# Branch A as seven block products, with its weights' forms and the output product's right operands made behind the first FFN, in a hybrid encoder layer

## The chip, the cores and the metric

The kernel runs on one core of one Trainium2 chip. The metric is device time in microseconds (us) for one execution of the whole layer; a run's span is the time from its first to its last instruction, and some microseconds lie around it. Engines are named as the profile names them: PE (TensorE, matrix products), DVE (VectorE), ACT (ScalarE), POOL (GpSimd) and SP (SyncE, which only issues transfers here).

## What is computed

One bidirectional encoder layer on 1024 tokens of width 1024, all in FP32:

```python
h = h + 0.5 * swiglu(rms_norm(h, ffn1_norm), w_gate1, w_up1, w_down1)
u = rms_norm(h, mix_norm)
qa, ka, va, qb, kb, vb, ga, gb = split(u @ w_in)
ya = neighbourhood_attention_2d(qa, ka, va, rpb)     # 8 heads of 64
yb = windowed_gqa_sink(qb, kb, vb, sink)             # 8 heads of 64
merged = sigmoid(ga) * (ya @ w_branch_a) + sigmoid(gb) * (yb @ w_branch_b)
h = h + merged @ w_out
h = h + 0.5 * swiglu(rms_norm(h, ffn2_norm), w_gate2, w_up2, w_down2)
return rms_norm(h, final_norm)
```

The change concerns `ya @ w_branch_a` (1024 tokens, 512 in, 1024 out: "branch A") and `merged @ w_out` (1024 x 1024 x 1024: "the output product").

## The kernel before

**Exact products from rounded operands.** PE multiplies FP32R operands. Each FP32 operand is split in two: ACT casts it to FP32R (hi, L95) and DVE subtracts that from the source (lo, L98). One product is then three matmuls (mm3, L146): hi times hi (L149), hi times lo (L151), lo times hi (L153), all accumulating in one PSUM bank. Such a product always needs a hi and a lo of both sides. The long products (the FFNs, the output product) are done as seven block products of halves with sums and differences of the blocks as operands ("forms", named P1 to P7), so that seven products do the work of eight.

**Stages in the order of the trace.** FFN 1 (the macaron half-step) up to about 432 us; its down product (class Down, L532); a transition; the input projection; from 935 us attention in 64 units (scores, turn, values; loop at L1476), and between the units' matmuls a "filler" (L1321) of gate columns, branch B and the first part of branch A; after 1160.5 us the rest of branch A (L1537); at 1195.94 us the output product (Down with n=4, L1525); then FFN 2 from about 1300 us to the end. PE runs without a break through all of them, taking each product's operands as the other engines make them. Every engine takes its own instructions strictly in the order that the program gives.

**Branch A before.** yA, a [512, 1024] matrix of (channel, token), comes in four row chunks. Each unit writes its outputs to a DRAM buffer or to a tile (L1381 copy on ACT, L1382 and L1392 adds on DVE). Three chunks are fetched back and split whole (L1496, 128x1024 each), the last one in halves (L1394). For each of eight output chunks dc (order p, p+4) branch_a takes four channel chunks times mm3 times two banks of 512 tokens: 24 matmuls of 128x512, 192 in all. Then DVE multiplies by the gate (L1557, twice 512) and adds to branch B's part (L1558, 1024 wide) in merged(dc). combine (L1528) makes the output product's left forms by four DVE operations (L1534) per p and stores them.

**The output product before.** Down.prep (L579) makes one of 28 entries: a left form (from merged or from left_d) and a right form (blocks of w_out, loaded whole to SBUF, with differences at L590 to L595), and splits each: two ACT casts and two DVE subtractions of 512 an entry. Six entries (RING) are prepared ahead. multiply (L616) takes four column groups, twelve matmuls an entry.

**Behind FFN 1.** PE's 153 block products of FFN 1 are numbered down to n=0 at the end. After each, behind_ffn1 (L770) does background work: the weights of branch B (8 pieces), of branch A (8) and of six gate columns (12 halves) are fetched (256 KB), split (ACT L760, DVE L761) into buffers of the ring "hs" (6), and put to DRAM by POOL's queue (two of 256 KB, L768), one piece every third n from n=100. The same hook drives FFN 1's own down product (Down.at_end, L607): its blocks are loaded at n=10 and 6, its first entries made at n=4, 2, 0. SP issues all loads in order; a load that waits for its buffer holds up those behind it.

## Time and profile before

| quantity | value |
|---|---|
| median of 3 runs | 1919.72 us (1918.26 to 1920.03) |
| span of the profiled execution | 1915.6 us; the median lies 4.1 us above it |
| mean granted clock of PE | 0.999 |
| busy share of the span | PE 99%, DVE 76%, ACT 49%, POOL 16% |
| chain that ended last | PE 97%, DVE 1%, DMA 1% |
| moved by DMA | 338.57 MB, mean 177 GB/s |

In the views a row of a timeline has its start, the duration, the engine, the line, the operation, output<-inputs and the shape; the idle time of the engine before it and what released it stand in brackets. A duration covers the whole pass through an engine, and the next instruction can start before it ends: the distance from one start to the next is what an instruction costs in a row of them. Of matmuls above all only that distance counts.

### The profile page before, as it was taken

To read this page: it belongs to the slowest core of one execution; us is meant where nothing else is said; L and a number is where in the kernel's file an instruction comes from. 1 tells how busy PE (TensorE), PEld (TensorE's weight loads), DVE (VectorE), ACT (ScalarE), POOL (GpSimd) and SP (SyncE) were. 2 spreads that over 40 slices of the span, in tenths; PEclk is the share of its full clock that TensorE was granted. 3 is DMA by queue.
4 is the path that set the end of the run, shared out by engine and by line. 5 is a ranking of instruction groups with operands and counts; after the bars stand their busy time and mean duration, and the time that the engine had idled before them with its cause. 6 is when DMAs were issued, how large, how long until landed. Compare 5 with 4: busy or idle time off the path is not lost.

```text
span 1915.6 us, 25959 instructions
## 1 busy us (share of the span) xinstructions
PE 1905.7 (99%) x9044; PEld 1597.7 (83%) x9044; DVE 1451.9 (76%) x2545; ACT 947.5 (49%) x1847; POOL 306.5 (16%) x477
## 2 busy tenths in 40 slices
PE   9999999999999999999999999999999999999998
PEld 7888888888888888898898888888888888888886
DVE  8988766668967778755887997999675566569864
ACT  7533444444446543444888983475333333344453
POOL 0012222214400112211112201010110001005111
PEclk9999999999999999999999999999999999999999
DMA  7256656677354277753648978444432323492341
GB/s 269 95 175 217 231 200 219 205 277 284 115 180 141 105 213 236 226 176 127 176 117 228 283 225 309 171 154 133 142 110 97 118 88 110 157 357 86 119 140 61
DMA packets 174211, 338.57 MB, mean 177 GB/s; under 512 B 17280, under 2 KB 79616, under 8 KB 174080
## 3 DMA queue, kind: packets, MB, share of 16 engines
q1 hardware_dynamic: 140752, 235.18, 37.5%
q0 software_dynamic: 32464, 100.69, 15.6%
q8 instruction: 71, 1.16, 0.3%
q10 hardware_dynamic: 864, 1.05, 0.2%
q14 instruction: 60, 0.49, 0.1%
HBM read 230.43 MB, written 108.19 MB: 177 GB/s over the span
## 4 chain that ended last, share of the span: by engine, by line
PE 97%; DVE 1%; DMA 1%; ACT 0%; issue 0%; POOL 0%; SPq 0%; POOLq 0%; DVEq 0%; ACTq 0%
PE g L149 18%; PE g L153 17%; PE g L151 17%; PE d L153 12%; PE d L151 12%; PE d L149 12%; PE d L1438 2%; PE g L1457 1%; PE d L1417 1%; PE g L1452 1%; PE d L1418 1%; PE d L142 1%; DVE ar L98 0%; DMA fx<-in_xt_dram 0%; DMA fx<-v_d 0%
## 5 line engine op out<-in xcount | busy, mean ns | idle before, releaser
L149 PE MATMUL g<-ar,ws 128*128 128x512 f32 x1064 | 404.6, 393 | 0.0
L151 PE MATMUL g<-ar,ws 128*128 128x512 f32 x1064 | 401.8, 390 | 0.0
L153 PE MATMUL g<-ar,ws 128*128 128x512 f32 x1064 | 400.4, 390 | 0.0
L149 PE MATMUL d<-ar,ws 128*128 128x512 f32 x728 | 281.6, 390 | 0.4 <-ACT ar L908 0.4
L151 PE MATMUL d<-ar,ws 128*128 128x512 f32 x728 | 281.1, 389 | 0.6 <-DVE ar L910 0.6
L153 PE MATMUL d<-ar,ws 128*128 128x512 f32 x728 | 281.2, 389 | 0.0
L153 PEld LDWEIGHTS g<-ar,ws 128*128 128x128 f32 x1064 | 199.6, 188 | 41.6
L151 PEld LDWEIGHTS g<-ar,ws 128*128 128x128 f32 x1064 | 199.6, 188 | 41.0
L149 PEld LDWEIGHTS g<-ar,ws 128*128 128x128 f32 x1064 | 196.6, 188 | 35.9 <-DVE fa L1030 0.3
L332 DVE TENSOR_TENSOR ws<-raw,ws 128x512 fp32r<-128x512 f32 x216 | 147.6, 688 | 92.9 <-ACT ws L325 92.0
L325 ACT CAST ws<-raw 128x512 fp32r<-128x512 f32 x216 | 132.6, 620 | 149.6 <-PE g L153 67.0
L151 PEld LDWEIGHTS d<-ar,ws 128*128 128x128 f32 x728 | 136.7, 188 | 29.8 <-DVE ar L910 1.2
L149 PEld LDWEIGHTS d<-ar,ws 128*128 128x128 f32 x728 | 136.5, 188 | 28.9 <-ACT ar L908 0.9
L153 PEld LDWEIGHTS d<-ar,ws 128*128 128x128 f32 x728 | 136.6, 188 | 28.7 <-DVE ws L332 0.5
L95 ACT CAST ws<-raw 128x512 fp32r<-128x512 f32 x98 | 61.0, 623 | 119.2 <-PE d L153 59.9
L98 DVE TENSOR_TENSOR ws<-raw,ws 128x512 fp32r<-128x512 f32 x98 | 73.2, 747 | 44.3 <-ACT ws L95 44.2
L444 POOL DMA_DIRECT2D hid<-fx x91 | 49.2, 540 | 349.6 <-DVE fx L504 221.6
L98 DVE TENSOR_TENSOR ws<-ar,ws 128x512 fp32r<-128x512 f32 x114 | 93.5, 828 | 14.6 <-ACT ws L95 14.6
L95 ACT CAST ar<-raw 128x512 fp32r<-128x512 f32 (+1 forms) x81 | 54.0, 670 | 83.5 <-PE g L151 51.5
L149 PE MATMUL g<-ws,ws 128*128 128x512 f32 x232 | 90.9, 392 | 0.0
L153 PE MATMUL g<-ws,ws 128*128 128x512 f32 x232 | 90.4, 390 | 0.0
L151 PE MATMUL g<-ws,ws 128*128 128x512 f32 x232 | 90.3, 389 | 0.0
(344 smaller groups left out, 3830.9 us busy)
## 6 DMA issues: line engine op xcount, KB each, us to landing
raw<-hid SPq DMA_DIRECT2D x70, 512.0 KB
hid<-fx POOLq DMA_DIRECT2D x91, 256.0 KB, 2.7
ar<-in_ffn_w_down_dram SPq DMA_DIRECT2D x32, 512.0 KB
raw<-in_ffn_w_up_dram SPq DMA_DIRECT2D x31, 512.0 KB
raw<-in_ffn_w_gate_dram SPq DMA_DIRECT2D x27, 512.0 KB
hid<-fa POOLq DMA_DIRECT2D x51, 256.0 KB, 2.7
ar<-zs_d POOLq DMA_DIRECT2D x48, 256.0 KB, 7.5
raw<-in_w_in_dram SPq DMA_DIRECT2D x20, 512.0 KB
```

The lines of the kernel that those rows point to most:

```text
L95: hi = nc.scalar.copy(dst_hi, src)
L98: (eng or nc.vector).tensor_tensor(dst_lo, src, f32v(dst_hi), op=ALU.subtract)
L142: nc.tensor.transpose(pt[:, c * P:(c + 1) * P], xs[:, (half * 4 + c) * P:(half * 4 + c + 1) * P], ident)
L149: nc.tensor.matmul(b, lhs[0], r[0], start=first, stop=False, **kw)
L151: nc.tensor.matmul(b, lhs[0], r[1], start=False, stop=False, **kw)
L153: nc.tensor.matmul(b, lhs[1], r[0], start=False, stop=last, **kw)
L325: nc.scalar.copy(w[0][:, :512], a)
L332: nc.vector.tensor_tensor(w[0][:, 512:], a, f32v(w[0][:, :512]), op=ALU.subtract)
L444: nc.gpsimd.dma_start(hid[PRODUCTS.index(p), i], src)
L1417: nc.tensor.matmul(b[:, :nw], un["q"][s], un["kd"][s][:, k0 * P:k1 * P], start=True, stop=False)
L1418: nc.tensor.matmul(b[:, :nw], un["q"][s], un["kl"][s][:, k0 * P:k1 * P], start=False, stop=True)
L1438: nc.tensor.transpose(pt[:, i * P:(i + 1) * P], un["pr"][s][:, i * P:(i + 1) * P], ident)
```

## The change

**Branch A in seven products.** The output chunks are taken in four pairs p (dc = p and p+4); tokens, channels and output columns are halved, and a pair takes seven block products of two channel chunks each, with one bank of 512: 7 x 2 x 3 = 42 matmuls of 128x512 a pair, 168 in all instead of 192. The first products (P1, P5 and P2 of p=0 and 1) lie in the filler, as the first part of branch A did; PE's sequence is the same as before up to the attention's tail. The right side now needs forms of yA: 14 splits of 128x512 (form) and 8 differences (minus, L1356 of the changed file) where there were three splits of 1024 and two of 512. A product that several outputs share is kept: ACT copies it from PSUM (a_keep, L1406, 12 times), DVE adds it (a_gate, L1414, 12 times), and then the gate is applied (L1416, 16 times as L1557 before) and merged (L1418, 8 times as L1558 before). combine has moved from L1534 to L1691.

**Weights' forms.** Branch A's weight forms (four pieces a pair) and the 28 right operands of the output product are made and split behind FFN 1 and put to DRAM (wa_d, wo_d). The output product's entries fetch their right operand, hi and lo in one transfer of 512 KB, instead of making it. The background is now a table of what follows each n: branch B and gates every second n from n=108; branch A's from n=67; the output product's from n=44, every 1.34 n, the last near n=6. Three buffers, the two "xs" and the one "gain", go round for the pieces.

The core of the diff:

```diff
+            if self.right is not None:
+                i = (e + self.shift) % self.RING
+                s, t = (ws4(), ws4()) if i < 4 else pair_slots(self.ring[i - 4])
+                nc.sync.dma_start(f32v(t), self.right[PRODUCTS.index(k), p])
+                split(s[:, :512], s[:, 512:], left, None, self.late)
+                self.ent[e] = s, t
+                return
...
+    def split_out(key, src):
+        n = src.shape[1]
+        o = cast[key] = halves_out()[:, :2 * n]
+        pin(nc.scalar.copy(o[:, :n], src))
+        pin(nc.vector.tensor_tensor(o[:, n:], src, f32v(o[:, :n]), op=ALU.subtract))
...
+    def wo_fetch(p):
+        for n, (r0, c0) in dict(B21=(4, 0), B11=(0, 0), B22=(4, 512), B12=(0, 512)).items():
+            wo[n, p] = hs(F32)
+            nc.sync.dma_start(wo[n, p], wout[0][(r0 + p) * P:(r0 + p + 1) * P, c0:c0 + 512])
+    def wo_split(k, p):
+        for d, a, b in dict(P5=(("B11", "B12", "B11"),), P7=(("B12", "B22", "B12"),), P6=(("B11", "B22", "B11"),),
+                            P4=(("B21", "B21", "B11"),)).get(k, ()):
+            pin(nc.vector.tensor_tensor(wo[d, p], wo[a, p], wo[b, p], op=ALU.subtract))
+        split_out((k, p), wo[SOURCE[k], p])
...
+    def wa_split(g, p):
+        lo, hi = slice(0, 256), slice(256, 512)
+        r1, r2 = wa_raw[p, 0], wa_raw[p, 1]
+        if g == 1:
+            q = wa_raw[p, 2] = hs(F32)
+            pin(nc.vector.tensor_tensor(q[:, lo], r2[:, lo], r2[:, hi], op=ALU.add))
+            pin(nc.vector.tensor_tensor(q[:, hi], r1[:, lo], r2[:, lo], op=ALU.subtract))
+        if g == 2:
+            q = wa_raw[p, 2]
+            pin(nc.vector.tensor_tensor(r1[:, lo], q[:, lo], r1[:, lo], op=ALU.subtract))
+            pin(nc.vector.tensor_tensor(r1[:, hi], r1[:, hi], r1[:, lo], op=ALU.subtract))
+        split_out((g, p), (r1, wa_raw[p, 2] if g == 1 else None, r1, r2[:, hi])[g])
...
+    for i in range(NC8 + 2 * len(gates)):
+        for e, f in ((3, wab_put), (2, wab_split), (0, wab_fetch)):
+            later(108 - 2 * i - e, f, i)
+    for p in range(4):
+        later(67 - 5 * p, wa_fetch, p)
+        for g in range(4):
+            later(64 - 5 * p - 5 * g // 4, wa_split, g, p)
+            later(63 - 5 * p - 5 * g // 4, wa_put, g, p)
+    step = [44 - 1.34 * k for k in range(29)]
+    for p in range(4):
+        later(step[7 * p] + 2, wo_fetch, p)
+        for j, k in enumerate(("P2", "P1", "P3", "P5", "P7", "P6", "P4")):
+            later(step[7 * p + j], wo_split, k, p)
+            later(step[7 * p + j] - 1, wo_put, k, p)
...
-        for e, f in ((3, wab_put), (2, wab_split), (0, wab_fetch)):
-            i, k = divmod(100 - e - n, 3)
-            if k == 0 and 0 <= i < 2 * (NC8 + len(gates)):
-                f(i)
+        for f, *a in background.get(n, ()):
+            f(*a)
...
+    def form(k, c, src):
+        h, l = [slot(i)[:, c * 512:c * 512 + 512] for i in FORMS[k]]
+        split(h, l, src, None, True)
+    def forms_first(c):
+        r = mix["ya", c]
+        form("P1", c, r[:, L])
+        minus(r[:, L], r[:, R], r[:, L])
+        form("P5", c, r[:, L])
+    def forms_last(c, k):
+        r, y = mix["ya", c], mix["ya", c + 2]
+        d, a, b, f = dict(P6=(r[:, L], y[:, R], r[:, L], r[:, L]), P7=(r[:, R], y[:, R], r[:, R], r[:, R]),
+                          P4=(y[:, L], y[:, L], r[:, L], y[:, L]), P3=(None, None, None, y[:, R]))[k]
+        if d is not None:
+            minus(d, a, b)
+        form(k, c, f)
...
+    def a_product(p, k):
+        g, f = GROUP[k]
+        w = mix["wa", p, g]
+        n = 256 if g == 3 else 512
+        key = "X" if k == "P2" else "Y" if k in ("P5", "P3") else "W"
+        first = k in ("P1", "P2", "P5")
+        if first:
+            bk[key, p] = bank("d" if key == "Y" else "g")
+        for c in range(2):
+            o = f * 256 + c * P
+            mm3([bk[key, p]], first and c == 0, c == 1, (w[:, o:o + P], w[:, n + o:n + o + P]),
+                [[slot(i)[:, c * 512:c * 512 + 512] for i in FORMS[k]]], skip_group_check=True)
+    def a_keep(p, k):
+        if k == "P1":
+            both = xs4()
+            kept_a[p, "P1"], kept_a[p, "P5"] = both[:, L], both[:, R]
+        elif k == "P6":
+            kept_a[p, "P6"] = hs(F32)
+        nc.scalar.copy(kept_a[p, k], bk["Y" if k == "P5" else "W", p])
+    def a_gate(p, k):
+        key, add, dc, n = dict(P2=("X", "P1", p, L), P7=("W", "P5", p + 4, R), P4=("W", None, p + 4, L), P3=("Y", "P6", p, R))[k]
+        src, r = bk[key, p], mix["ra", dc]
+        if add is not None:
+            t = kept_a[p, add]
+            nc.vector.tensor_tensor(t, src, t, op=ALU.add)
+            src = t
+        nc.vector.scalar_tensor_tensor(out=r[:, n], in0=r[:, n], scalar=1.0, in1=src, op0=ALU.add, op1=ALU.mult)
+        if k in ("P4", "P3"):
+            nc.vector.tensor_tensor(merged(dc), merged(dc), r, op=ALU.add)
...
+        for k, p, g, f in (("P1", 0, 0, "P6"), ("P5", 0, 1, "P7"), ("P1", 1, None, "P3"), ("P5", 1, None, "P4")):
+            a_product(p, k)
+            yield
+            a_keep(p, k)
+            if g is not None:
+                fetch_wa(1, g)
+            forms_last(0, f)
+            if p == 0 and k == "P5":
+                a_fetch(0)
+        a_open(0)
+        for p in range(2):
+            a_product(p, "P2")
+            yield
+            fetch_wa(p, 2)
...
-            fetch_y(512 + min(n - 57, 2) * P)
-        if n in (60, 61, 63):
-            split_y(Y_A[min(n - 60, 2)], 512 + min(n - 60, 2) * P, nc.vector)
+            fetch_ya(min(n - 57, 2))
+        if n in (60, 61):
+            forms_first(n - 60)
+        if n == 63:
+            form("P2", 0, mix["ya", 2][:, L])
...
+    for k in ("P6", "P3", "P7", "P4"):
+        forms_last(1, k)
...
-    down = Down(4, wo[0], 0.5, place, quarter, {k: left_d[i] for i, k in enumerate(("P5", "P6", "P3", "P7"))},
-                loads, (8, 10), late=True)
+    down = Down(4, None, 0.5, {}, quarter, {k: left_d[i] for i, k in enumerate(("P5", "P6", "P3", "P7"))},
+                loads, (8, 10), late=True, right=wo_d)
...
-    for i, dc in enumerate(a_order):
...
+    def both(p, *ks):
+        for k in ks:
+            for q in (p, p + 1):
+                a_product(q, k)
+                if k in ("P1", "P5", "P6"):
+                    a_keep(q, k)
+    def weights(p, g):
+        for q in (p, p + 1):
+            fetch_wa(q, g)
+    weights(0, 3)
+    a_fetch(1)
+    for p in (0, 2):
+        if p:
+            both(p, "P1", "P5")
+            a_open(3)
+            combine(0)
+            both(p, "P2")
+            combine(1)
+        both(p, "P6")
+        if p == 0:
+            a_open(1)
+            weights(2, 0)
+        for q in (p, p + 1):
+            a_gate(q, "P2")
+        both(p, "P3")
+        if p == 0:
+            weights(2, 1)
+        both(p, "P7")
+        if p == 0:
+            weights(2, 2)
+        for q in (p, p + 1):
+            a_gate(q, "P3")
+            a_gate(q, "P7")
+        both(p, "P4")
+        if p == 0:
+            weights(2, 3)
+        for q in (p, p + 1):
+            a_gate(q, "P4")
+            if p == 0:
+                a_fetch(q + 2)
+        if p == 0:
+            a_open(2)
+            for t in range(4):
+                new_fx(t)
             new_ar(2)
-        if i + 1 == NC8:
-            down.prep_until(2)
...
+    down.prep_until(2)
+    for p in (2, 3):
+        combine(p)
```

Three places of the new order, as the engines' queues hold it. A row names the line, operation, output<-inputs and shape, and what it waits for; numbers behind names tell tiles apart. DVE at the end of attention, before. The rows L1382 and L1392 write the last two units' outputs; ar_564 is the lo of the last part of yA (from fx_10503), on which PE's next lo product waits:

```order
L1382 TENSOR_TENSOR s_839_7519<-g_10804,s_839_7519 64x256 [waits Activation_49]
L1392 TENSOR_TENSOR fx_10503<-g_10804,s_839_7519 64x128 [waits DVE_49]
L1392 TENSOR_TENSOR fx_10503<-g_10804,s_839_7519 64x128
L1382 TENSOR_TENSOR s_839_7519<-g_10831,s_839_7519 64x256 [waits Activation_49]
L1392 TENSOR_TENSOR fx_10503<-g_10831,s_839_7519 64x128 [waits DVE_49]
L1392 TENSOR_TENSOR fx_10503<-g_10831,s_839_7519 64x128
L98 TENSOR_TENSOR ar_564<-fx_10503,ar_564 128x512 [waits Activation_49]
L1557 SCALAR_TENSOR_TENSOR raw_10759<-raw_10759,d_10735 128x512 [waits PE_49,Activation_49]
```

The same place in the changed program. ar_4921 and ar_5300 (higher up) hold forms of yA, xs_10960 and xs_11014 are kept products, raw_10991 a gate, and the last row makes P6's form of the second channel chunk from fx_10701:

```order
L98 TENSOR_TENSOR ar_5300<-fx_10744,ar_5300 128x512 [waits Activation_49]
L1540 TENSOR_TENSOR s_887_7717<-g_11025,s_887_7717 64x256 [waits Activation_49]
L1356 TENSOR_TENSOR fx_10744<-fx_10744,raw_10592 128x512
L1550 TENSOR_TENSOR fx_10701<-g_11025,s_887_7717 64x128 [waits DVE_49]
L1550 TENSOR_TENSOR fx_10701<-g_11025,s_887_7717 64x128
L1414 TENSOR_TENSOR xs_10960<-g_11042,xs_10960 128x512 [waits DMASW2_49,PE_49]
L98 TENSOR_TENSOR ar_5300<-fx_10744,ar_5300 128x512 [waits Activation_49]
L1416 SCALAR_TENSOR_TENSOR raw_10991<-raw_10991,xs_10960 128x512 [waits DVE_49,Activation_49]
L1414 TENSOR_TENSOR xs_11014<-g_11051,xs_11014 128x512 [waits PE_49]
L1540 TENSOR_TENSOR s_887_7717<-g_11058,s_887_7717 64x256 [waits Activation_49]
L1550 TENSOR_TENSOR fx_10701<-g_11058,s_887_7717 64x128 [waits DVE_49]
L1550 TENSOR_TENSOR fx_10701<-g_11058,s_887_7717 64x128
L1356 TENSOR_TENSOR raw_10638<-fx_10701,raw_10638 128x512 [waits DVE_49]
```

Between the last units' adds there now stand L1356, a form's lo (L98), two adds of kept products (L1414) and a gate (L1416), ahead of the last unit's add and of the first difference that needs it (raw_10638). On PE its cast is awaited by the first L149 of P6's second chunk (the third L149 row here), twelve rows behind the last unit's values:

```order
L149 MATMUL d_10967<-ar_5300,ws_11049 128x512
L151 MATMUL d_10967<-ar_5300,ws_11049 128x512
L153 MATMUL d_10967<-ar_5300,ws_11049 128x512
L149 MATMUL d_11018<-ar_5300,ws_11067 128x512
L151 MATMUL d_11018<-ar_5300,ws_11067 128x512
L153 MATMUL d_11018<-ar_5300,ws_11067 128x512
L149 MATMUL g_10939<-ar_4921,ws_11049 128x512 [waits Activation_49]
L149 MATMUL g_10995<-ar_4921,ws_11067 128x512
```

DVE where branch A ends and the output product begins, before. ws_11075 and ws_11081 are the lo's of the left forms of the first two entries, ws_11076 and ws_11082 of the right ones; raw_10926 is a gate:

```order
L1558 TENSOR_TENSOR ar_9540<-ar_9540,raw_10892 128x1024 [waits DVE_49]
L1534 TENSOR_TENSOR fa<-ar_9540 128x512 [waits DMASW0_49,DVE_49]
L98 TENSOR_TENSOR ws_11075<-ar_9541,ws_11075 128x512 [waits DMAHW0_49,Activation_49]
L98 TENSOR_TENSOR ws_11076<-ar_10855,ws_11076 128x512 [waits DMAHW6_49,DMAHW1_49,Activation_49]
L98 TENSOR_TENSOR ws_11081<-ar_9541,ws_11081 128x512 [waits DMAHW3_49,Activation_49]
L98 TENSOR_TENSOR ws_11082<-ar_10855,ws_11082 128x512 [waits DMAHW6_49,Activation_49]
L1557 SCALAR_TENSOR_TENSOR raw_10926<-raw_10926,g_11003 128x512 [waits PE_49]
L1557 SCALAR_TENSOR_TENSOR raw_10926<-raw_10926,g_11004 128x512 [waits PE_49]
L1558 TENSOR_TENSOR ar_9541<-ar_9541,raw_10926 128x1024 [waits DVE_49]
```

The same place in the changed program, with the left forms' lo's ws_11328 and ws_11333:

```order
L1418 TENSOR_TENSOR ar_9738<-ar_9738,raw_11181 128x1024 [waits DVE_49]
L1416 SCALAR_TENSOR_TENSOR raw_11183<-raw_11183,xs_11208 128x512 [waits DVE_49,Activation_49]
L1416 SCALAR_TENSOR_TENSOR raw_11177<-raw_11177,g_11192 128x512 [waits PE_49]
L1416 SCALAR_TENSOR_TENSOR raw_11183<-raw_11183,g_11201 128x512 [waits PE_49]
L1418 TENSOR_TENSOR ar_9739<-ar_9739,raw_11177 128x1024 [waits DVE_49]
L1418 TENSOR_TENSOR ar_9739<-ar_9739,raw_11183 128x1024 [waits DVE_49]
L98 TENSOR_TENSOR ws_11328<-ar_9739,ws_11328 128x512 [waits DMAHW0_49]
L98 TENSOR_TENSOR ws_11333<-ar_9739,ws_11333 128x512 [waits DMAHW6_49,DMAHW1_49,Activation_49]
L1691 TENSOR_TENSOR fa<-ar_9738,ar_9739 128x512 [waits DMASW4_49,DVE_49]
```

The first entries' lo's have moved behind the last gates and merges, and the third entry's lo (ws_11367, not shown) behind all eight combine operations of p=2 and 3 (L1691), of which the last row is the first. PE there, changed program; g_11201 is the last product of branch A (P4 of p=3), d_11356 to d_11359 the output product's first banks, and ws_11328's lo is first used at the L153 row:

```order
L153 MATMUL g_11201<-ar_5300,ws_11171 128x512
L149 MATMUL g_11201<-ar_5300,ws_11171 128x512
L151 MATMUL g_11201<-ar_5300,ws_11171 128x512
L153 MATMUL g_11201<-ar_5300,ws_11171 128x512
L149 MATMUL d_11359<-ws_11329,ws_11328 128x512
L151 MATMUL d_11359<-ws_11329,ws_11328 128x512
L153 MATMUL d_11356<-ws_11329,ws_11328 128x512 [waits DVE_49]
L153 MATMUL d_11357<-ws_11329,ws_11328 128x512
L153 MATMUL d_11358<-ws_11329,ws_11328 128x512
L153 MATMUL d_11359<-ws_11329,ws_11328 128x512
```

Two matmuls stand between branch A's last product and the wait for the lo; before, the output product's first row was itself the wait, but its lo's were made ahead of the last gates.

121 lines of the change are left out of this document (61 added, 60 removed).

## The prediction

> **What bounds the kernel now.** I read the page first, then what PE waited for, then the windows stage by stage, then the DVE and PE timelines at the two places where the order changes.
>
> ```profile
> span 1915.6 us, 25959 instructions
> PE 97%; DVE 1%; DMA 1%; ACT 0%; issue 0%; POOL 0%; SPq 0%; POOLq 0%; DVEq 0%; ACTq 0%
> ```
>
> The chain that ended last is PE itself, and the view of PE's waits names only these:
>
> ```profile
> PE g L829 <- POOL ident masks.py:199: 1.5, 1, 1.5
> PE d L151 <- DVE ar L910: 0.6, 2, 0.3
> PE d L149 <- ACT ar L908: 0.4, 1, 0.4
> PE d L1438 <- DVE ws L98: 0.2, 1, 0.2
> ```
>
> So hardly anything can be won here by making PE wait less; a change pays by fewer matmuls, and loses what it makes PE wait. The windows give the price of a matmul and show how busy the helpers are (columns: window, length, busy time and count of PE, PEld, DVE, ACT, POOL, the granted clock, DMA share, GB/s):
>
> ```profile
> 0.00:20.00 20.00, 17.42 (x90) 14.28 (x91) 11.81 (x19) 14.49 (x25) 1.91 (x10) 1.00 0.89 329
> 20.00:100.00 80.00, 80.00 (x356) 66.23 (x355) 76.12 (x126) 46.64 (x83) 5.47 (x8) 1.00 0.38 139
> 200.00:300.00 100.00, 100.00 (x443) 82.81 (x442) 70.50 (x111) 44.10 (x78) 23.64 (x44) 1.00 0.66 227
> 300.00:400.00 100.00, 100.00 (x443) 82.81 (x442) 69.61 (x108) 41.91 (x74) 22.67 (x42) 1.00 0.59 195
> 400.00:420.00 20.00, 20.00 (x90) 16.57 (x89) 6.83 (x10) 7.25 (x13) 0.54 (x1) 1.00 1.00 368
> 1136.00:1164.00 28.00, 28.00 (x157) 23.68 (x157) 22.72 (x60) 18.01 (x41) 0.00 (x0) 1.00 0.82 299
> 1196.00:1258.00 62.00, 62.00 (x274) 51.10 (x273) 61.82 (x100) 29.85 (x54) 5.30 (x9) 1.00 0.53 187
> 1700.00:1800.00 100.00, 100.00 (x443) 82.81 (x442) 90.86 (x109) 41.53 (x73) 37.42 (x24) 1.00 0.47 163
> ```
>
> 443 matmuls in 100 us are 0.2257 us each; in the output product it is 62/274 = 0.2263, which I take. DVE is full in the output product (61.82 of 62 us), which still runs without a gap.
>
> **Branch A's matmuls.** 192 become 168: 24 x 0.2263 = 5.43 us less. This is the only gain on PE, and it is sure as long as PE isn't kept waiting.
>
> **The tail of attention.** The timeline of DVE before, with the last values on PE and the last cast on ACT:
>
> ```profile
> 1136.17 1.23 DVE L98 TENSOR_TENSOR ar<-raw,ar 128x1024 fp32r<-128x1024 f32 x1
> ...
> 1157.71 0.42 DVE L1382 TENSOR_TENSOR s<-g,s 64x256 f32<-64x256 f32 x1 [1.44 <-ACT s L1381]
> ...
> 1160.93 0.42 DVE L1382 TENSOR_TENSOR s<-g,s 64x256 f32<-64x256 f32 x1 [2.19 <-ACT s L1381]
> 1161.38 0.58 DVE L1392 TENSOR_TENSOR fx<-g,s 64x128 f32<-64x128 f32 x2
> 1162.65 0.69 DVE L98 TENSOR_TENSOR ar<-fx,ar 128x512 fp32r<-128x512 f32 x1 [0.69 <-ACT ar L95]
> ```
> ```profile
> 1160.33 0.40 PE L149 MATMUL d<-ar,ws 128*128 128x512 f32 x1
> ...
> 1162.00 0.62 ACT L95 CAST ar<-fx 128x512 fp32r<-128x512 f32 x1 [1.09 <-DVE fx L1392]
> ```
>
> From the first split of yA to the end of the last one, 1136.17 to 1163.34, are 27.2 us, in which DVE idles 1.44 + 2.19 + 0.69 = 4.3: 22.9 us of work. What an operation costs in a row of them shows where they follow each other without idle time:
>
> ```profile
> 1141.39 1.23 DVE L98 TENSOR_TENSOR ar<-raw,ar 128x1024 fp32r<-128x1024 f32 x1
> 1142.54 0.68 DVE L1310 SCALAR_TENSOR_TENSOR ar<-masks,g 128x512 f32<-128x512 f32 x1
> ...
> 1194.20 0.68 DVE L1534 TENSOR_TENSOR fa<-fa,ar 128x512 f32<-128x512 f32 x1
> 1194.80 0.69 DVE L98 TENSOR_TENSOR ws<-ar,ws 128x512 fp32r<-128x512 f32 x1
> 1195.40 0.69 DVE L1534 TENSOR_TENSOR fa<-ar,fa 128x512 f32<-128x512 f32 x1
> ```
>
> One of 512 takes 0.60 us from start to start, at a duration of 0.68 to 0.69 (0.605 where I sum many); one of 1024 takes 1.15.
>
> Before, the forms of yA were three of 1024 and two of 512 in that stretch: 3 x 1.15 + 2 x 0.60 = 4.65 us. In the new order, up to the first difference that needs the last unit (the last row of its fence above), there stand ten splits of 512, six differences, two adds of kept products and one gate: 19 x 0.605 = 11.5 us. DVE thus has 22.9 - 4.65 + 11.5 = 29.7 us to do from 1136.17: it is at 1165.9 where PE, with the same rows ahead of the last values, is at 1160.33 plus twelve matmuls = 1163.05. With the cast (0.62) P6's second chunk is there at 1166.5: PE waits 3.45 us, and some 0.15 more for the lo. The 4.3 us in which DVE idled are the cover, and they are used up. As a lower bound DVE's start could come earlier than 1136.17 (in that window it had 22.72 of 28 us): I take 0 as the least, and 5 as the most, if ACT is late as well (18.01 of 28 us busy, and four copies of kept products and some five more casts to come, of about 0.6 us each).
>
> The Trainium skill speaks to that price: in "VectorE: DVE Perf Modes", "The DRAIN you can't avoid", the next operation doesn't start until the pipe is empty. By it 512 columns would cost their duration, 0.69 instead of 0.605, the stretch's 23 operations of that width 2 us more, and the stall would be 5.5. The starts 0.60 apart in this trace speak against it, and I keep to them.
>
> **The seam into the output product.** Before, DVE had the first entries' lo's behind it well ahead of the last gates:
>
> ```profile
> 1187.90 2.50 DVE L98 TENSOR_TENSOR ws<-ar,ws 128x512 fp32r<-128x512 f32 x4 [4.96 <-ACT ws L95]
> ...
> 1199.18 1.28 DVE L1557 SCALAR_TENSOR_TENSOR raw<-raw,g 128x512 f32<-128x512 f32 x2
> 1200.49 1.23 DVE L1558 TENSOR_TENSOR ar<-ar,raw 128x1024 f32<-128x1024 f32 x1
> ```
> ```profile
> 1195.49 0.61 PE L153 MATMUL g<-ar,ws 128*128 128x512 f32 x2
> 1195.94 0.39 PE L149 MATMUL d<-ws,ws 128*128 128x512 f32 x1
> ...
> 1204.10 0.39 PE L149 MATMUL d<-ws,ws 128*128 128x512 f32 x1
> 1204.40 0.50 PE L151 MATMUL d<-ws,ws 128*128 128x512 f32 x1
> ```
>
> Now the lo of the first entry stands behind the gate of the last product. From that product's end DVE has the gate (0.62), two merges of 1024 (1.15 to 1.26 each) and the lo (0.69), with the hand-offs 3.8 us, while PE has two matmuls left, 0.45: a wait of 3.35 us, or up to 4.0 if the gate before it is still undone then. I take 3.6. Behind it the third entry's lo stands after eight combine operations. When PE goes on, DVE has one lo, eight operations and the lo to do, 0.6 + 4.8 + 0.69 = 6.1 us, and PE 19 matmuls, 4.3: another 1.7 us. Nothing else is late there: the same rows for p=0 and 1 lie beside two more products' matmuls (168 against 192 spread over the same gates). The seam costs 5.3 us (5.0 to 5.7). Its least is 0 only if branch A itself ends with DVE ahead, which the dependence on the last product excludes for the first 3.35.
>
> **The output product.** 28 casts, 28 lo's and 16 differences leave it. They are off the path: PE's waits name no line of it, and of its rows only the L151 at 1204.40 comes late, 0.30 behind the L149 before it instead of 0.2263. For such small gaps here and in the transition behind it I give 0.3 us back (0 to 0.6). The right operands now come by DMA, 28 x 0.52 = 14.7 MB over some 76 us, 190 GB/s on the row's 187. That is 377, near the 368 of the fullest row above. Six entries are fetched ahead, 6 x 12 x 0.2263 = 16 us, so a transfer can be late by that much at no cost.
>
> **Behind FFN 1.** DVE gets the differences and splits: in one iteration of FFN 1 (14 products of 2.72 us, 38 us) at most 18 more than the 42 of the rows above. That is 70 + 18 x 0.605/0.381 = 99% if all are of 512; 15 are half as wide, which leaves some 85 to 90%. The rows 20 to 100 (76.12 of 80) and 1700 to 1800 (90.86) show PE without a gap beside as full a DVE. By DMA come, from 312 to 418 us, 28 pieces of 512 KB and 16 of 256 KB, 18.9 MB, 180 GB/s on 195, less the gate pieces that have moved forward (768 KB per 8.2 us, 95 GB/s, for most of that stretch): some 290 GB/s, under the 368 of the row 400 to 420. In that row the queue is full, and about 2.3 MB fall into it. I take 0.3 us; from 0 to 8, the upper end being a transfer that holds an in-order engine (below).
>
> **The sum.** -5.43 + 3.6 + 5.3 - 0.3 + 0.3 = +3.5 us. The profiled execution's span of 1915.6 and the 4.1 us around it make the median, 1919.72: 1923.2 us. The least a measurement can tell here from no change is about 0.2%, 3.84 us, so this lies just within it.
>
> **The rivals.**
>
> *A, the stalls are mostly hidden.* If DVE starts the forms earlier, the tail's stall goes (-3.6); with only the first seam wait left, -5.43 + 3.4 - 0.3 = -2.3, 1917.4 us, and with that halved by a lucky order of the last gates 1915.5. For it: DVE had 5.3 us free in the 28 of the tail. Against: the queue order is fixed, and the free time lies behind the splits, where it waited for the last units. The change doing what it says, -5.43 in full, would be 1914.3. Chance 0.22.
>
> *B, slower: the queue at the end of FFN 1.* FFN 1's down product loads some 5 MB from n=10 on (405 us), in the row with DMA share 1.00. If the 512 KB pieces take half of that rate while they last (to 418), its first entries come 5 to 7 us later. ACT, waiting there for the data in order, then holds up its copies of finished products (P6's to an SBUF tile, 2.72 us ahead of PE's need of the bank), and PE stands for what exceeds that, 2.5 to 4 us. The same can happen at every piece whose buffer is still being put away. It decides from the point where a wait on ACT or DVE in FFN 1 exceeds the 2.72 us of one product; with two or three such waits +6, 1929. For it: the share of 1.00 and only three buffers in rotation. Against: the average above, and no wait of PE in the rows of FFN 1 today. Chance 0.21.
>
> *C, the right operands arrive late in the output product* (377 asked against 368 given): 62 us at 2% short are 1.5 us, inside the 16 ahead; only if the transition's loads queue behind them does PE wait, some 2 us: 1925. Chance 0.05.
>
> *D, the clock falls in the waits.* Two waits of 3.5 us are new for PE. If the clock were halved after one for as long again, each would cost 3.5 / 2 = 1.7 us more: 1926.6. The first row of the windows has 2.6 us without a matmul and a clock of 1.00, so no fall is seen from a pause of that size. The Trainium skill has the rule, "TensorE: Matmul & The Clock Gate", "What's actually happening": an idle window of about 3.4 us, free-running, throttles the array to half. No run here yet shows a pause long enough. Chance 0.04.
>
> **How the numbers follow.** The forecast, two waits of DVE's making that take back the matmuls' gain and a little more, has 0.48; its own range is 1918.7 to 1926, from the tail (0 to 5), the seam (5.0 to 5.7) and the small terms. To hold 8 in 10 the whole range reaches into A and takes in most of B: 1915.0 to 1929.5. Within 0.2%: 0.30 of the forecast (below 1923.56), 0.07 of A (its 1917.4), 0.02 of B and 0.01 of C, 0.40. Faster: the 0.15 of A below 1915.9. Slower: the rest, 0.18 of the forecast, 0.19 of B, 0.04 of C and 0.04 of D, 0.45.
>
> **What would show it.** Right: in the changed profile, PE waits at P6's second chunk for ACT's cast (L95), 3 to 4 us, about 7 us after the last values; a second wait at the first L153 of the output product for DVE's lo (L98), 3.3 to 4 us, and a third of 1 to 2 us two entries later; DVE without idle time in the tail; the output product's DVE well under 100% busy. Wrong: no wait in the tail (then A), or waits of PE for ACT or DVE between 140 and 435 us (then B), or in the output product on DMA (C), or a granted clock under 0.99 right behind a wait (D).

## The result, and the profile after

The changed kernel takes 1930.73 us (median of 5 runs, 1927.95 to 1931.02) against 1919.09 for the kernel before in the same session (5 runs): a ratio of 1.0061, 95% interval 1.0049 to 1.0072. It is slower by 0.6%, outside the range forecast. The profiled execution's span is 1926.2 us, 10.6 more than before. It is that of the fastest of the five runs; the spans of the other four are 2.0 to 3.0 us longer, and no trace shows where. First the page, then what PE waited for:

```profile
span 1926.2 us, 26199 instructions
PE 85%; DVE 5%; issue 4%; DMA 4%; POOL 1%; ACT 0%; SPq 0%; POOLq 0%; DVEq 0%; ACTq 0%
```
```profile
PE d L153 <- DVE ws L98: 3.7, 1, 3.7
PE d L151 <- DVE ws L98: 1.9, 2, 1.6
PE g L913 <- POOL ident masks.py:199: 1.5, 1, 1.5
PE g L149 <- ACT fx L477: 1.5, 1, 1.5
PE g L149 <- ACT ar L95: 1.5, 2, 1.3
PE d L151 <- DVE ar L98: 1.0, 1, 1.0
PE d L1597 <- DVE ws L98: 0.8, 2, 0.6
```

Only the POOL row stood there before. To see where the time went I took the start of the same matmul in both traces: up to the attention's tail PE's sequence is the same, so the n-th from the start is the same one, and behind branch A the n-th from the end. The table, called the ledger below, has the growth of the difference, stage by stage, in us, and what the prediction's sum had for it:

| stage | measured | predicted |
|---|---|---|
| FFN 1, to 430 us | +1.96 | } |
| FFN 1's down product, 430 to 545 us | +4.06 | } +0.3 for all three |
| 545 to 1075 us | +0.91 | } |
| tail, branch A, output product, the rest | +3.20 | -5.43 + 3.6 + 5.3 - 0.3 = +3.2 |
| to the last matmul | +10.1 | +3.5 |

So the part that was worked out from the order came out to a tenth in sum (its terms did not, see below), and the term that was taken as nearly nothing is the whole error.

**FFN 1.** ACT and PE around 224 us (timeline):

```profile
223.97 0.62 ACT L768 CAST hs<-hs 128x512 fp32r<-128x512 f32 x1 [4.66 <-DMA hs<-in_w_in_dram]
224.49 0.58 ACT L477 COPY fx<-g 128x512 f32<-128x512 f32 x1
```
```profile
225.12 0.50 PE L149 MATMUL g<-ar,ws 128*128 128x512 f32 x1 [1.52 <-ACT fx L477]
```

ACT stood 4.66 us for a background piece of a gate's weights, with the copy of a finished product queued behind it; that copy frees the bank that PE wants next. Two fetches of such pieces had been issued close behind each other, at 216.31 and 217.47, and the first took 7.56 us to land. By the trace SP had been held before them: 4.3 us, to 208.0, for a buffer of the ring "hs" (released by DVE's L769), then 7.0 us, to 215.9, for the buffers of two loads of FFN 1's own weights (released by DVE's L332).

**FFN 1's down product.** The windows by stage, after (columns as in the prediction):

```profile
312.00:400.00 88.00, 88.00 (x390) 72.86 (x389) 77.65 (x127) 44.84 (x79) 24.27 (x45) 1.00 0.78 287
400.00:420.00 20.00, 20.00 (x90) 16.55 (x89) 11.94 (x19) 9.58 (x18) 2.68 (x5) 1.00 1.02 374
460.00:480.00 20.00, 20.00 (x90) 16.56 (x89) 19.89 (x27) 8.97 (x16) 11.86 (x5) 1.00 1.00 370
```
```profile
468.14 16.72 POOL L601 TENSOR_TENSOR ar<-ar,ar 128x512 f32<-128x512 f32 x7 [27.12 <-PE g L153]
```
```profile
513.82 1.67 DVE L600 TENSOR_TENSOR ar<-xs,ar 128x512 f32<-128x512 f32 x1
515.42 1.78 DVE L98 TENSOR_TENSOR ws<-raw,ws 128x512 fp32r<-128x512 f32 x1
517.12 1.75 DVE L98 TENSOR_TENSOR ws<-ar,ws 128x512 fp32r<-128x512 f32 x1
```

Before, the same things read so:

```profile
460.00:480.00 20.00, 20.00 (x90) 16.57 (x89) 19.93 (x24) 8.78 (x16) 16.50 (x9) 1.00 0.41 135
```
```profile
457.00 7.84 POOL L593 TENSOR_TENSOR ar<-ar,ar 128x512 f32<-128x512 f32 x5 [23.58 <-DMA raw<-hid]
```
```profile
472.51 1.66 DVE L590 TENSOR_TENSOR ar<-ar,ar 128x512 f32<-128x512 f32 x1
474.09 1.79 DVE L98 TENSOR_TENSOR ws<-raw,ws 128x512 fp32r<-128x512 f32 x1
475.80 1.78 DVE L98 TENSOR_TENSOR ws<-ar,ws 128x512 fp32r<-128x512 f32 x1
```

From 312 to 400 us the transfers come to 287 GB/s, as worked out (290). But the DMA engines, full from 400 to about 460 us before, are now full to 480. The blocks of w_down, from which POOL makes FFN 1's differences (L601, L593 before), land late: POOL begins at 468.1 instead of 457.0, 9 us later as seen from PE (1.96 of the 11.1 is PE's own delay). The row names a PE matmul as what ended POOL's wait; but by the trace's semaphore events the block of w_down that POOL waited for landed at 467.9 us, and at 456.8 before. A POOL subtraction takes 1.4 to 1.75 us there, the first one 6.5 (before, one took 5.3), and a DVE row beside it 1.7 instead of 0.68, in both kernels. DVE is busy 19.9 of 20 us from 460 to 520 us, as it was before from 460, so the delay is not made up, and PE waits at 517 and 522 us, 1.6 and 1.0 us by the trace. The long DVE rows beside POOL's are what the Trainium skill describes in "SBUF — State Buffer", "Who interferes with whom": a DVE instruction with two SBUF inputs contends with a GpSimd instruction that reads SBUF.

**The tail.** PE's waits there are 0.63 at 1161.33 (for a lo of DVE's) and this one, with 0.17 at P6's second chunk, where 3.45 had been forecast:

```profile
1167.92 0.47 PE L149 MATMUL g<-ar,ws 128*128 128x512 f32 x1 [1.31 <-ACT ar L95]
...
1172.93 0.73 PE L149 MATMUL g<-ar,ws 128*128 128x512 f32 x2 [0.17 <-ACT ar L95]
```

With small steps beside them the ledger has 3.1 us for the tail, the 24 matmuls saved not counted. The wait at 1167.92 is the start of P2 for p=1, which takes a PSUM bank that the last unit but one had: DVE's two adds of that unit (L1550) ran from 1167.21 to 1167.78. The cast that the row names ended at 1167.94, when the matmul had begun, so it is not what PE waited for. DVE was late, as forecast, but PE met it earlier, at a bank.

**The seam.** PE, and the windows around it:

```profile
1202.16 0.39 PE L151 MATMUL d<-ws,ws 128*128 128x512 f32 x1
1206.22 1.61 PE L153 MATMUL d<-ws,ws 128*128 128x512 f32 x4 [3.68 <-DVE ws L98]
1207.64 0.63 PE L149 MATMUL d<-ws,ws 128*128 128x512 f32 x1
1208.06 0.63 PE L151 MATMUL d<-ws,ws 128*128 128x512 f32 x1
```
```profile
1202.00:1206.50 4.50, 0.82 (x4) 0.40 (x3) 4.50 (x7) 1.47 (x3) 0.00 (x0) 1.00 1.03 415
1206.50:1210.00 3.50, 3.50 (x10) 2.72 (x10) 3.50 (x7) 1.42 (x3) 2.15 (x4) 0.54 0.83 298
```

The wait is the forecast one, 3.8 us against 3.6. Behind it the granted clock is 0.54 for 3.5 us and the matmuls come every 0.43 us: the mechanism of rival D, at 1.6 us. It took the place of the third wait (1.7 us, for the third entry's lo), since eight slow matmuls gave DVE the time; e9_pitch1 below shows the third wait where the clock did not fall.

### The profile page after: what moved, and what is told of

The parts are those of the page before. It is cut to its first block, busy times and chain, and to the rows that moved or that the text cites. A ratio compares the mean times of both kernels' runs of the same rounds, so it can differ in the third digit from the quotient of the medians.

```text
span 1926.2 us, 26199 instructions
## 1 busy us (share of the span) xinstructions
PE 1905.3 (99%) x9020; PEld 1594.1 (83%) x9020; DVE 1474.7 (77%) x2598; ACT 961.4 (50%) x1876; POOL 323.6 (17%) x505
## 4 chain that ended last, share of the span: by engine, by line
PE 85%; DVE 5%; issue 4%; DMA 4%; POOL 1%; ACT 0%; SPq 0%; POOLq 0%; DVEq 0%; ACTq 0%
PE g L149 16%; PE g L151 16%; PE g L153 16%; PE d L153 10%; PE d L151 10%; PE d L149 10%; PE d L1597 2%; DVE ws L98 1%; PE g L1616 1%; PE d L1576 1%; PE d L1577 1%; PE g L1611 1%; DVE ar L98 1%; DMA ar<-in_ffn_w_down_dram 1%; DMA raw<-hid 1%
## 5 line engine op out<-in xcount | busy, mean ns | idle before, releaser
L149 PE MATMUL g<-ar,ws 128*128 128x512 f32 x1072 | 410.3, 394 | 3.5 <-ACT fx L477 1.5
L151 PE MATMUL g<-ar,ws 128*128 128x512 f32 x1072 | 407.4, 390 | 0.0
L153 PE MATMUL g<-ar,ws 128*128 128x512 f32 x1072 | 406.0, 390 | 0.0
L151 PE MATMUL d<-ar,ws 128*128 128x512 f32 x712 | 277.3, 389 | 0.6 <-DVE ar L994 0.6
L149 PE MATMUL d<-ar,ws 128*128 128x512 f32 x712 | 277.6, 390 | 0.2 <-ACT ar L992 0.2
L153 PE MATMUL d<-ar,ws 128*128 128x512 f32 x712 | 277.2, 389 | 0.0
L153 PEld LDWEIGHTS g<-ar,ws 128*128 128x128 f32 x1072 | 201.1, 188 | 41.9
L149 PEld LDWEIGHTS g<-ar,ws 128*128 128x128 f32 x1072 | 198.2, 188 | 41.9 <-issue 2.6
L332 DVE TENSOR_TENSOR ws<-raw,ws 128x512 fp32r<-128x512 f32 x216 | 147.6, 688 | 80.5 <-ACT ws L325 79.9
L151 PEld LDWEIGHTS d<-ar,ws 128*128 128x128 f32 x712 | 133.7, 188 | 28.9 <-DVE ar L994 1.2
L149 PEld LDWEIGHTS d<-ar,ws 128*128 128x128 f32 x712 | 133.6, 188 | 28.3 <-ACT ar L992 0.8
L153 PEld LDWEIGHTS d<-ar,ws 128*128 128x128 f32 x712 | 133.7, 188 | 27.9 <-DVE ws L332 0.4
L98 DVE TENSOR_TENSOR ws<-raw,ws 128x512 fp32r<-128x512 f32 x98 | 73.5, 752 | 39.4 <-ACT ws L95 39.4
L98 DVE TENSOR_TENSOR ws<-ar,ws 128x512 fp32r<-128x512 f32 x94 | 79.5, 848 | 16.1 <-ACT ws L95 16.0
L149 PE MATMUL g<-ws,ws 128*128 128x512 f32 x232 | 90.9, 392 | 0.0
L153 PE MATMUL g<-ws,ws 128*128 128x512 f32 x232 | 90.4, 390 | 0.0
```

The lines of the kernel that those rows point to most:

```text
L98: (eng or nc.vector).tensor_tensor(dst_lo, src, f32v(dst_hi), op=ALU.subtract)
L149: nc.tensor.matmul(b, lhs[0], r[0], start=first, stop=False, **kw)
L151: nc.tensor.matmul(b, lhs[0], r[1], start=False, stop=False, **kw)
L153: nc.tensor.matmul(b, lhs[1], r[0], start=False, stop=last, **kw)
L332: nc.vector.tensor_tensor(w[0][:, 512:], a, f32v(w[0][:, :512]), op=ALU.subtract)
```

## The experiments

Ten kernels. Each was timed beside the kernel before; the ratio is to that, with its 95% interval. The ledger is by the same matmul's start as above (the first 20 us of a run differ by up to 0.7 us from one execution to the next and lie in the first column). Each row is one execution. Until about 305 us e1, e2, e3, e8 and e9 run the change's own program, and e3, e8 and e9 do so again from 545 to 1075 us: what differs there between them is chance.

| run | ratio | FFN 1 | 430 to 545 | 545 to 1075 | the rest |
|---|---|---|---|---|---|
| the change | 1.0061 (1.0049 to 1.0072) | 1.96 | 4.06 | 0.91 | 3.20 |
| e1_no_wo | 1.0025 (1.0015 to 1.0034) | 0.81 | 0.00 | 0.01 | 3.25 |
| e2_no_put | 1.0037 (1.0023 to 1.0052) | 1.23 | 1.31 | 0.33 | 4.77 |
| e3_seam | 1.0054 (1.0039 to 1.0069) | 3.45 | 4.64 | -0.04 | 2.07 |
| e4_shift14 | 1.0042 (1.0027 to 1.0057) | 4.22 | 0.00 | 0.30 | 3.85 |
| e5_a_good | 1.0049 (1.0034 to 1.0064) | 2.79 | 0.62 | 0.12 | 3.83 |
| e6_all | 1.0046 (1.0029 to 1.0062) | 3.82 | 0.00 | 0.06 | 4.40 |
| e7_wo_only | 1.0031 (1.0018 to 1.0044) | 0.73 | 4.22 | 0.10 | -0.17 |
| e8_seam_tail | 1.0056 (1.0041 to 1.0071) | 1.97 | 3.66 | 0.01 | 3.97 |
| e9_pitch1 | 1.0087 (1.0071 to 1.0102) | 9.50 | 2.09 | -0.07 | 3.03 |
| e10_forms | 1.0029 (1.0018 to 1.0040) | -0.69 | 2.65 | 0.00 | 5.89 |

The theory after the result was: the transfers behind FFN 1 are late at its end and delay the down product, and DVE's order makes the waits at the tail and the seam. The rival: the casts and subtractions behind FFN 1 are what costs, or DVE's amount of work rather than its order.

### e1_no_wo and e2_no_put: the transfers or the work?

```diff
-        later(step[7 * p] + 2, wo_fetch, p)
...
-            later(step[7 * p + j], wo_split, k, p)
-            later(step[7 * p + j] - 1, wo_put, k, p)
-                nc.sync.dma_start(f32v(t), self.right[PRODUCTS.index(k), p])
+                nc.sync.dma_start(f32v(t), wb_d[(e + 1) % NC8])
```

> The changed kernel without the output product's right operands behind FFN 1: they are neither made nor put away, and its entries fetch 512 KB pieces of branch B's weights in their place, so the output product is not that of w_out. If the work behind FFN 1 causes the waits of PE at 440 us (0.5) and 517 to 525 us (3.5), both go: about 1926.5 us, POOL's differences of FFN 1's down product start near 458 us again, and the waits at 225 us (1.8), in the tail (2.6) and at the seam (5.6 with the slow clock behind it) stay. If those waits came from the later start of something else, it stays at 1930.

In e2_no_put only the line of wo_put goes, and the fetch is replaced as well.

> As the kernel without the right operands, but they are fetched, formed and split behind FFN 1 as in the changed kernel and only not put to DRAM (14.7 MB less); the output product's entries fetch pieces of branch B's weights. If it is the transfers that delay FFN 1's down product, it is as fast as without the whole work, 1926.5 us, DMA share well under 1.00 after 460 us. If it is the casts and subtractions on ACT and DVE, it is as the changed kernel, 1930.

Without the operands the waits at 440 and 517 us are gone to the hundredth, and POOL begins at 457.0. e1_no_wo came out at 1922.5, 4 us better than expected. The ledger has 1.15 of it in FFN 1, where the wait at 224 us lies before all that the edit touches, and 0.90 behind 545 us, where the 0.6 at 751 us are missing, as in e3, e8 and e9: both are chance of one execution. Another 1.4 is the session, in which the kernel before took 1917.73. PE's waits in e1_no_wo:

```profile
PE d L153 <- DVE ws L98: 3.7, 1, 3.7
...
PE g L149 <- ACT ar L95: 1.3, 1, 1.3
PE g L149 <- ACT fx L477: 0.9, 1, 0.9
PE d L1592 <- DVE ws L98: 0.8, 2, 0.6
```

With all the work and only the puts away, 430 to 545 us costs 1.31 instead of 4.06: two thirds go with the transfers out. The last third is what the fetches, or the blocks of w_down that load into the two "xs" buffers (at 223 us before, at 469 us after, since the pieces hold these buffers until then), still delay; these two were not told apart. The 4.77 in e2's last column is the seam's slow clock, which lasted twice as long here: 0.54 on average over the 7.5 us from 1201.5.

### e3_seam: the order at the seam

```diff
         both(p, "P4")
+        if p:
+            down.prep_until(2)
...
-    down.prep_until(2)
+    down.prep_until(4)
     for p in (2, 3):
         combine(p)
```

> The changed kernel with the output product's first two entries made ahead of the last gates, and the next two ahead of the last combines. If DVE's order makes the wait at the seam and the wait makes the clock fall, the 3.8 us wait and the 1.6 us of slow clock both go: about 1925 us, granted clock 1.00 in all windows. If the wait only moves to the next lo, 1928 to 1929.

The wait and the slow clock went: 0.34 us is left of the 3.84, and the granted clock stays at 1.00.

```profile
1202.00:1206.50 4.50, 4.33 (x19) 3.21 (x19) 4.50 (x7) 0.00 (x0) 0.00 (x0) 1.00 1.03 415
1206.50:1210.00 3.50, 3.50 (x17) 2.83 (x16) 3.50 (x6) 2.76 (x6) 0.54 (x1) 1.00 1.03 417
```

But the rest fell only from 3.20 to 2.07, because new waits came. Three are for right operands, 0.56, 1.10 and 0.85 us by the starts:

```profile
1210.86 0.47 PE L149 MATMUL d<-ws,ws 128*128 128x512 f32 x1 [0.40 <-DMA ws<-wo_d]
...
1231.13 0.47 PE L149 MATMUL d<-ar 128*128 128x512 f32 x1 [0.95 <-DMA ar<-wo_d]
...
1237.55 0.47 PE L149 MATMUL g<-ws,ws 128*128 128x512 f32 x1 [0.69 <-DMA ws<-wo_d]
```

This is what rival C had: with PE on time the right operands are late, and in the changed kernel the pause at the seam had given them the time. It is not the whole account, since e7_wo_only below fetches the same operands, has no pause and no such wait; what the new branch A adds to it stays open. Another 1.25 us is lost around the start of FFN 2 (1297 to 1311 us), of which the trace names 0.5 as a wait for DVE (L332). In this run FFN 1 cost 1.5 us more by chance of its waits, so the time hardly moved.

### e4_shift14: the same work, 38 us earlier

```diff
-            later(108 - 2 * i - e, f, i)
+            later(122 - 2 * i - e, f, i)
...
-        later(67 - 5 * p, wa_fetch, p)
+        later(81 - 5 * p, wa_fetch, p)
...
-    step = [44 - 1.34 * k for k in range(29)]
+    step = [58 - 1.34 * k for k in range(29)]
```

(and wa_split and wa_put by 14 too)

> The changed kernel with the whole background behind FFN 1 begun 14 products (38 us) earlier, so that it ends near 380 us instead of 418. If the collision is with the loads of FFN 1's down product from 405 us on, the waits at 440 and 517 us go: about 1926.5 us. If it is the amount of work, the waits move to FFN 1's fuller beginning (DVE 95% busy up to 100 us) and it is 1930 or slower.

Both answers at once: 430 to 545 us costs nothing, so the down product feels the place of the background and not its amount (the four blocks for "xs" load at 381 to 387 us here, so this run does not tell the two causes left open above apart), and a new wait of 3.5 us stands at 158 us, for which the trace names a DVE row (L479) of FFN 1's finished products. FFN 1 itself uses the ring "hs" up to about there.

### e9_pitch1: the same work, denser

```diff
-    step = [44 - 1.34 * k for k in range(29)]
+    step = [44 - 1.0 * k for k in range(29)]
```

> The changed kernel with the output product's right operands made every product from n=44 instead of every 1.34, so that the last is put away near n=16 (388 us) and not n=6 (416 us); nothing else is moved. If the collision with the loads of FFN 1's down product (from 405 us) makes the waits at 440 and 517 us, they go and the wait at 225 us stays: 4 us less than the changed kernel, 7 to 8 us above before. If the denser work holds up FFN 1 instead, waits of PE between 312 and 400 us and no gain.

The second answer: 430 to 545 us halves, but FFN 1 waits for ACT's copies at 342 and 345 us. It does so at 223 us too, 2.9 us, where the program is still that of the change (1.7 there). The pauses at 223 and 345 us have a slow clock behind them:

```profile
PE g L149 <- ACT fx L477: 2.7, 1, 2.7
PE g L149 <- ACT fa L477: 2.7, 2, 2.0
```
```profile
340.00:348.00 8.00, 5.32 (x23) 3.77 (x22) 2.66 (x5) 3.24 (x6) 0.91 (x2) 1.00 1.01 400
348.00:352.00 4.00, 4.00 (x12) 3.17 (x11) 3.87 (x7) 2.46 (x5) 0.69 (x2) 0.58 0.62 251
```

It also shows the third wait of the seam: here the clock did not fall behind the first, and 1.58 us came two entries later, where 1.7 had been forecast (by the trace 1.42):

```profile
1210.64 1.19 PE L153 MATMUL d<-ws,ws 128*128 128x512 f32 x4 [3.60 <-DVE ws L98]
...
1216.66 0.50 PE L153 MATMUL d<-ws,ws 128*128 128x512 f32 x1 [1.42 <-DVE ws L98]
```

### e7_wo_only: the operands without the new branch A

Branch A, its weights and the order around it are those of before; the background takes wo_fetch, wo_split and wo_put from the change, and Down its "right" branch.

```diff
-            i, k = divmod(100 - e - n, 3)
-            if k == 0 and 0 <= i < 2 * (NC8 + len(gates)):
-                f(i)
+        for f, *a in background.get(n, ()):
+            f(*a)
...
-            down.load_blocks(("B21", "B11", "B12", "B22")[i // 2])
...
-    down = Down(4, wo[0], 0.5, place, quarter, {k: left_d[i] for i, k in enumerate(("P5", "P6", "P3", "P7"))},
+    down = Down(4, None, 0.5, {}, quarter, {k: left_d[i] for i, k in enumerate(("P5", "P6", "P3", "P7"))},
```

> Branch A as before in eight products, with the output product's right operands made behind FFN 1 as in the change (branch B, A and gates every second product from n=108). If these operands are the costly half, it has the waits at 225, 440 and 517 us and none at the tail and the seam: 4 to 6 us slower than before, 1922 to 1924. If the 60 casts, lo's and differences taken from the output product are worth something there, 1 us less; if the cost needs the new branch A, as before, 1918.

The first answer: 4.2 us in the down product, and from 1075 us on it gains 0.17. Taking 72 operations off ACT, DVE and their queues there was worth no more than that (0.3 had been forecast), since PE had hardly waited for them. Its right operands arrive in time.

### e8_seam_tail, e5_a_good, e6_all: mending what can be mended

Beside the seam's order:

```diff
-        for k, p, g, f in (("P1", 0, 0, "P6"), ("P5", 0, 1, "P7"), ("P1", 1, None, "P3"), ("P5", 1, None, "P4")):
+        for k, p, g, f in (("P1", 0, 0, "P6"), ("P5", 0, 1, "P3"), ("P1", 1, None, None), ("P5", 1, None, None)):
...
-    for k in ("P6", "P3", "P7", "P4"):
-        forms_last(1, k)
+    for c, k in ((1, "P6"), (1, "P3"), (0, "P7"), (1, "P7"), (0, "P4"), (1, "P4")):
+        forms_last(c, k)
```

and the gates of P2 (p = 0 and 1) behind P3.

> The changed kernel with the seam's and the tail's order mended, the background behind FFN 1 as in the change. Against the run with the seam alone: if the tail's 2.6 us come from DVE's 2.4 us of forms that aren't needed yet ahead of the last units' adds, 1.5 to 2.5 us less, 1925.5 to 1926.5; if they come from the banks that branch A holds, no less, 1928.

> Seven products alone, in the best order found: without the output product's right operands behind FFN 1 (pieces of branch B's weights are fetched in their place), with the seam's order of the run before, with the tail's forms for P7 and P4 and the gates of P2 moved behind the last unit, and with branch B's and the gates' weights every third product from n=126. If the ledger of waits is complete, only the 24 matmuls are left: 5.4 us faster than before, less some tenths, 1912.5 to 1914 us against 1917.7. If DVE has too much to do for the seven products in any order, the waits move and it is no faster than 1917.

> The whole change with all mended: seam and tail as in the run before it, and the background behind FFN 1 begun earlier (branch B and gates every 2.5 products from n=128, the rest 12 products earlier). If the collisions of the transfers are the only cost left, the waits at 225, 440 and 517 us go and those for the right operands in the output product (1.6 us) stay: 1914 to 1916 us. If the background only moves its waits within FFN 1, 1918 to 1921.

None of the three did it. In e8_seam_tail the tail comes to 3.3 us instead of 3.1, spread over more places up to 1172, and 0.7 more at 1181; the rest went from e3's 2.07 to 3.97: 1.4 more for the right operands, 1.0 more in the tail, 0.6 less at the seam:

```profile
PE d L149 <- DMA ar<-wo_d: 2.3, 1, 2.3
...
PE g L149 <- DVE fx L1551: 0.9, 1, 0.9
PE d L1598 <- DVE ws L98: 0.8, 2, 0.6
PE g L149 <- DMA ws<-wo_d: 0.8, 1, 0.8
```

The row of L1551 (L1550 in the change) is the bank of the unit's adds, named outright here. From 1145 to 1160 us DVE is busy 14.7 of 15 us in the change and 14.8 in e8 (11.95 before), and ACT 13.5 and 13.7 (8.02 before): moving forms about does not make room. e5_a_good and e6_all add an earlier background, which brings the wait at 158 us again (3.2 and 3.1). In e6_all the largest wait of the tail is one for branch A's weights (DMA ws<-wa_d, 2.1 us at 1172, and 0.2 in e8); its cause is open. In e5_a_good 2.7 us of PE's waits are for the pieces fetched in place of the right operands (DMA from wb_d: 1.6, 0.8 and 0.3), so this run does not price the seven products beside the output product of before; that kernel was not run. In no order tried were the seven products faster than before.

### e10_forms: half the bytes

The output product splits its right operands itself, as before; only 16 forms are made behind FFN 1, unsplit.

```diff
+        if k in ("P1", "P2", "P3"):
+            r0, c0 = dict(P1=(0, 0), P2=(4, 0), P3=(4, 512))[k]
+            return wout[0][(r0 + p) * P:(r0 + p + 1) * P, c0:c0 + 512]
+        return wo_d[PRODUCTS.index(k), p, :, :512]
...
+            r = hs(F32)
+            nc.sync.dma_start(r, self.right(*self.seq[e]))
+            split(t[:, :512], t[:, 512:], r, None, self.late)
```

> Seam and tail mended, and the output product's right operands split where they are used, as before: behind FFN 1 only the 16 forms are made and put unsplit (4.2 MB instead of 14.7), the plain blocks are fetched from w_out, 256 KB an entry instead of 512; branch B's and the gates' weights every 2.5 products from n=100. If full transfers cause what is left, the waits in FFN 1, at 440 and 517 us and for the right operands in the output product (1.6 to 3.3 us) go; the tail (2 to 3 us) stays, and DVE is full again in the output product: -5.4 + 3 to 4, 1 to 2 us faster than before, 1916 to 1917. If DVE's splits there now come late, 1919 to 1922.

The second answer, and more: FFN 1 is free of waits and the right operands are never late, but the work it gives back to DVE is now in the way from 1160 us on (5.89 in the rest), with waits for DVE at the tail, one there for branch A's weights (1.3 us), and waits for DVE and ACT at the seam (1.4 and 1.7 us) and the transition (0.7 to 1.1, three times). Its forms come late in FFN 1, so the down product still loses 2.65. No version tried beats the kernel before.

## Why the prediction was wrong, point by point

**The matmuls, the tail, the seam, the output product: right in sum.** Forecast +3.2, measured +3.20. That it fits to a tenth is luck, since the parts are off and cancel: tail 3.6 against 3.1, met at a PSUM bank and not at the form; seam 5.3 against 5.7, as 3.8 + 1.6 of slow clock and small steps instead of 3.6 + 1.7; given back 0.3 against 0.2. The mechanism of rival D did come, but in the stead of the third wait. Of the signs named, the first wait of the seam and a DVE without idle time in the tail (0.16 us in all from 1156 to 1175) came; the 3 to 4 us at P6's second chunk and the third wait did not, and those of B (a wait for ACT at 224 us) and D (a clock of 0.54 behind a wait) did. e3_seam removes the seam's wait by making the entries earlier, fetch, cast and lo together, so it is shown that their place in the order makes it; that it is DVE's lo among these is named by the trace. That DVE's lateness makes the tail's wait is read from the trace; e8 did not remove it, and how it divides between DVE's work and the banks held by branch A stays open.

**Behind FFN 1: the step that failed.** "I take 0.3 us; from 0 to 8" measured 6.9: 1.96 in FFN 1, 4.06 in its down product, 0.91 behind. The 4.06 is the part that comes again (3.66 to 4.64 in e3, e7 and e8). With the same program in these stretches FFN 1 cost 3.45 in e3 and 1.97 in e8, and the 0.91 was -0.07 to 0.01 in e3, e8 and e9, so the 0.91 and the size of FFN 1's share are chance of one execution. Rival B had the place, the queue at the end of FFN 1, and with its 1929 nearly the time; it had 0.21. Where the step went wrong: it compared an average (290 GB/s) with a peak (368) over a stretch that ends in a full stretch. What doesn't fit before 405 us is not spread, it pushes the following loads back, and these were already at a share of 1.00. And it looked for the wait at the first entries; the late blocks went through POOL's differences and a full DVE, and PE waited only 50 us after POOL began. It also left out that the pieces hold the two "xs" buffers, so that four blocks of w_down loaded at 223 us before now load at 469 us, in the full stretch; what this alone costs is open. The runs show the dose (POOL's first difference late as seen from PE, and the cost from 430 to 545 us):

| run | POOL late, us | cost, us |
|---|---|---|
| e1, e4, e6 | -0.8, -0.1, 0.1 | 0.00 |
| e2_no_put | 2.9 | 1.31 |
| e9_pitch1 | 3.7 | 2.09 |
| e10_forms | 7.1 | 2.65 |
| e8, the change, e7, e3 | 8.8, 9.2, 9.7, 10.0 | 3.66, 4.06, 4.22, 4.64 |

(e5_a_good is outside it, 0.62 us with POOL early.) The wait at 224 us is a second part. The seven runs with pieces every second product from n=108 (the change, e1, e2, e3, e7, e8, e9) have it, 1.0 to 3.2 us; the kernel before, with every third, and e10_forms, with every 2.5, have none. That the spacing makes it is argued from this, and not shown by a run that changes nothing else.

**The rivals.** A did not come. C was latent: the right operands are late, at 0.4 to 2.3 us a wait, but only beside the new branch A and once the seam's pause is gone; the 377 GB/s asked for are not too much by themselves, since e7_wo_only has no such wait at a DMA share of 0.94 to 1.03 (1202 to 1232 us). The range ended at 1929.5, 1.2 us short: it took B at its 6 us, where the term's own upper end was 8.

## What to carry to other kernels

Work moved "behind" a stage must be checked against what follows that stage: ask not whether the average fits but at which point its last transfer lands, and what is queued there. Where the helper engines and the DMA are full on both sides of the place, moving work moves the waits: each wait mended here by another order or place (the seam in e3, the end of FFN 1 in e4 and e9) was followed by new ones of a like size, and only leaving the work out (e1) removed one for good. And taking work off an engine that was busy but hardly waited for gained 0.17 us.

## What the runs showed of the hardware

The granted clock of PE fell to about a half for some 3.5 us after waits of 3.8 us (the change, e1, e2, e4, all at the seam; in e2 for 6.8 us), but also after one of 2.9 us (0.50 from 226 to 229 us in e9_pitch1), one of 2.1 us close behind one of 0.9 (0.58, above) and one of 1.9 us (0.57 from 522 to 526 us in e3_seam); it did not after 3.8 us (e9's seam), 3.5 us (e4 at 158 us) and 3.2 us (e3 at 223 us). The Trainium skill, "TensorE: Matmul & The Clock Gate", "What's actually happening", has a free-running window of about 3.4 us, of which a whole one must be idle. The free phase would explain that waits of one length differ; that a wait of 1.9 us was enough it does not explain.
